# A grouped convolution: the first half image block by a plain load and a ScalarE cast, the weights on another queue

## Chip, cores, metric

One core of one Trainium2 chip. Times are device microseconds of a whole run. Every run told of here was "fast" (slow when it lies over 1.5% above the fastest of its kernel), and only such runs are compared. The sets of runs were made on chips 0, 3, 13 and 15; each set has the kernel before in its own rounds, and times are compared by the ratio to it.

## What must be computed

A 3x3 convolution in 8 groups, with padding of one pixel: x is 16 x 64 x 64 x 64, the weights are 128 x 8 x 3 x 3, the output is 16 x 128 x 64 x 64, all fp32.

```python
for g in range(8):
  for b in range(16):
    for co in range(16):
      for ci in range(8):
        for kh in range(3):
          for kw in range(3):
            output[b, 16*g + co] += weight[16*g + co, ci, kh, kw] * x_pad[b, 8*g + ci, kh:kh+64, kw:kw+64]
```

That is 16.8 MB to read and 33.6 MB to write.

## The kernel before

GpSimd issues all image loads, and they cast fp32 to bf16 on the way (16.81 MB read, 8.39 MB written by its queue, q0). SyncE issues the weights, and later the 32 stores of 1 MB. DVE multiplies the weights with a mask into E (five instructions); TensorE transposes E, DVE and ScalarE copy the result as bf16 to wN and wS. Then TensorE does two interleaved pipes of matmuls on 32x64 tiles, and ScalarE and DVE copy the filled banks to output buffers.

```python
    def load(t, row0, p0, p1, h0, h1):
        s = sem(f"ld{len(sems)}")
        nc.gpsimd.dma_start(                                  # fp32 in memory, bf16 in t: casts
            t.rearrange("p h w -> p (h w)")[p0:p1, h0 * W : h1 * W],
            xr[row0 + p0 : row0 + p1, h0 * W : h1 * W],
        ).then_inc(s, 16)
        # ... cut: landed[tile, quarter, row] = (s, 16)

    s_w = sem("w")
    nc.sync.dma_start(w_sb, weight.rearrange("co ci kh kw -> co (ci kh kw)")).then_inc(s_w, 16)
    # ... cut: memsets of mask and ident
    for h0, h1 in ((0, 32), (32, 64)):
        load(xn[0], 0, 0, 128, h0, h1)
        if h0 == 0:
            # ... cut: three affine_selects on GpSimd
        load(xs[0], 544, 0, 128, h0, h1)
        load(xs[3], 512 - 96, 96, 128, h0, h1)
    # ... cut: the other six tiles, whole

    DVE.wait((s_w, 16), m5)
    for r in range(5):
        # ... cut: e = DVE.done(tensor_mul(E part, weights, mask part))
    PE.wait(e, m4)
    # ... cut: transposes on TensorE, copies to wN (DVE) and wS (ScalarE); the matmuls

        def finish(self, st):
            # ... cut
                    eng.wait((stored[slot], 16 * uses[slot]) if uses[slot] else None, self.full[j, im])
                    free[b] = eng.done(copy(ob[slot][:, o0 : o0 + 512], banks[b]))
            # ... cut: after two sets, SyncE stores ob[slot]; 16 such buffers in rotation
```

Of the kernel before, what the change touches and what calls it, by code (L numbers as in the profile page):

```python
# [13 lines left out]
def kernel(  # L14
# [38 lines left out]
    with tc.tile_critical():  # L53
        program(nc, x, weight, out, xn, xs, ob, w_sb, mask, ident, E, wN, wS, banks)
# [29 lines left out]
def program(nc, x, weight, out, xn, xs, ob, w_sb, mask, ident, E, wN, wS, banks):  # L84
    H = W = 64
    HW, HALF, T, G, CIg, COg, R = H * W, H * W // 2, 9, 8, 8, 16, 8
    NOB = len(ob)
# [3 lines left out]
    ACT = Order(nc, nc.scalar, "act", sems)  # L91
# [3 lines left out]
    def sem(name):  # L95
        s = nc.alloc_semaphore(name)
        sems.append(s)
        return s


    xr = x.rearrange("b c h w -> (b c) (h w)")
    landed = {}

    def load(t, row0, p0, p1, h0, h1):
        s = sem(f"ld{len(sems)}")
        nc.gpsimd.dma_start(  # L106
# [3 lines that stand above are left out]
        for q in range(p0 // 32, p1 // 32):  # L110
            for h in range(h0, h1):
                landed[t.name, q, h] = (s, 16)

    s_w = sem("w")
    nc.sync.dma_start(w_sb, weight.rearrange("co ci kh kw -> co (ci kh kw)")).then_inc(s_w, 16)

    m1 = DVE.done(nc.vector.memset(mask, 1.0))  # L117
    m2 = DVE.done(nc.vector.memset(ident, 0.0))  # L118
    for h0, h1 in ((0, 32), (32, 64)):
        load(xn[0], 0, 0, 128, h0, h1)  # L120
        if h0 == 0:
            POOL.wait(m1)
            m3 = POOL.done(nc.gpsimd.affine_select(  # L123
                out=mask, in_=mask, compare_op=ALU.is_ge, fill=0.0,
                base=0, channel_multiplier=1, pattern=[[-COg, G]],
            ))
            POOL.wait(m2)
            m4 = POOL.done(nc.gpsimd.affine_select(  # L128
                out=ident, in_=ident, compare_op=ALU.not_equal, fill=1.0,
                base=0, channel_multiplier=1, pattern=[[-1, 128]],  # L130
            ))
            POOL.wait(m3)
            m5 = POOL.done(nc.gpsimd.affine_select(  # L133
                out=mask, in_=mask, compare_op=ALU.is_ge, fill=0.0,
                base=COg - 1, channel_multiplier=-1, pattern=[[COg, G]],
            ))
        load(xs[0], 544, 0, 128, h0, h1)
        load(xs[3], 512 - 96, 96, 128, h0, h1)
    for i in range(1, 4):
        load(xn[i], 128 * i, 0, 128, 0, H)  # L140
# [16 lines left out]
    for k, (wt, off) in enumerate(((wN, 0), (wS, 32))):  # L157
        for g, t0 in enumerate(range(0, T, 4)):
# [9 lines left out]
            p = PE.done(ins)  # L168
            dst = wt[:, t0 : t0 + n, :].rearrange("p t c -> p (t c)")
            eng, copy = ((DVE, nc.vector.tensor_copy), (ACT, nc.scalar.copy))[k]  # L170
# [11 lines left out]
    stored = [sem(f"st{i}") for i in range(NOB)]  # L182
    uses = [0] * NOB
# [3 lines left out]
    class Pipe:  # L187
# [53 lines left out]
        def finish(self, st):  # L241
            i, s = st // 4, st % 4
            if s % 2 == 0:
                self.slots = [(nob[0] + im) % NOB for im in range(2)]
                self.wrote = [[], []]
                nob[0] += 2
            for j in range(2):
                for im in range(2):
                    slot, b = self.slots[im], self.banks[j][im]
                    o0 = 512 * (2 * (s % 2) + j)  # L250
                    eng, copy = ((ACT, nc.scalar.copy), (DVE, nc.vector.tensor_copy))[nev[0] % 2]
                    nev[0] += 1
                    eng.wait((stored[slot], 16 * uses[slot]) if uses[slot] else None, self.full[j, im])
                    free[b] = eng.done(copy(ob[slot][:, o0 : o0 + 512], banks[b]))  # L254
                    self.wrote[im].append(free[b])
                nev[0] += 1
            nev[0] += 1
            if s % 2 == 1:
                s0 = HALF * (s // 2)
                for im in range(2):  # L260
                    slot = self.slots[im]
                    img = 2 * i + 8 * self.k + im
                    SP.wait(*self.wrote[im])
                    nc.sync.dma_start(outf[img][:, s0 : s0 + HALF], ob[slot]).then_inc(stored[slot], 16)
                    uses[slot] += 1
# [55 lines left out]
```

## Time and profile before

| | before |
|---|---|
| time, median of 3 runs | 130.17 us (130.03 to 130.27) |
| span of the profiled run | 128.2 us |
| TensorE busy | 86.9 us, done at 94 us |
| first convolution matmul | 7.92 us |
| stores issued | from 19.95 to about 99.3 us |

The page's slices tell when a unit is full. In answers of windows, each line has the stretch, its length, the busy time of five engines, TensorE's granted clock, the busy share of the 16 DMA engines, and the GB/s at the destination. A window counts each packet whole where it begins, so the edges of short windows are blurred, and shares slightly over 1 occur. The prediction shows the lines.

### The profile page before, as it was taken

The page shows a single profiled execution, that of the slowest core. Times are in us where ns is not written, and L with a number is a line of the kernel's source. Part 1 is how long each engine was busy: PE and PEld are TensorE (multiplying, and loading weights), DVE is VectorE, ACT ScalarE, POOL GpSimd, SP SyncE. Part 2 cuts the span into 40 slices and gives each one's busy share as a digit, 9 for nine tenths or more (in the row PEclk, how much of TensorE's full clock was granted, in tenths as well). Part 3 has the DMA queues.
Part 4 walks back from the last instruction along what each step waited for, and adds up shares of the span by engine and source line. Part 5 has one row for each costly group of instructions (what it writes and reads, how often), then busy time and mean ns, then how long its engine had stood idle before and what let it go on. Part 6 is the DMA issues. An engine that isn't in the chain of part 4 may idle for free.

```text
span 128.2 us, 3808 instructions
## 1 busy us (share of the span) xinstructions
PE 86.9 (68%) x2322; PEld 41.2 (32%) x1170; DVE 45.8 (36%) x74; ACT 37.0 (29%) x68; POOL 7.2 (6%) x19
## 2 busy tenths in 40 slices
PE   0199999999999999999999999999910000000000
PEld 0153353544435355444553544544500000000000
DVE  1840465446444645446544564465440000000000
ACT  4030354345333543336333453354330000000000
POOL 5960000000000000000000000000000000000000
PEclk9999999999999999999999999999996555555555
DMA  2999999999999999999999999999999999999950
GB/s 24 162 202 215 224 212 220 215 289 284 281 289 281 284 271 297 297 401 424 419 424 424 396 435 406 435 414 429 417 424 429 424 432 422 429 427 432 427 243 10
DMA packets 6271, 42.21 MB, mean 329 GB/s; under 512 B 848, under 2 KB 848, under 8 KB 1424
## 3 DMA queue, kind: packets, MB, share of 16 engines
q1 hardware_dynamic: 4752, 33.59, 62.9%
q0 software_dynamic: 1504, 8.39, 32.8%
q8 instruction: 13, 0.21, 0.6%
q14 instruction: 2, 0.02, 0.0%
HBM read 16.81 MB, written 33.55 MB: 393 GB/s over the span
## 4 chain that ended last, share of the span: by engine, by line
PE 67%; DVE 4%; issue 2%; POOL 1%; POOLq 0%; DVEq 0%; SPq 0%
PE bank L227 65%; DVE E L149 2%; DVE ob L254 2%; PE bank L162 2%; POOL ident L128 0%; POOL mask L123 0%; POOL mask L133 0%; POOL xn L106 0%; POOLq L123 0%; POOLq L316 0%; DVEq L75 0%; SPq L53 0%
## 5 line engine op out<-in xcount | busy, mean ns | idle before, releaser
L227 PE MATMUL bank<-xs,wS 32*64 32x504 bf16 (+3 forms) x1152 | 71.6, 374 | 0.6 <-issue 0.4
L227 PE MATMUL bank<-xn,wN 32*64 32x504 bf16 (+3 forms) x1152 | 71.8, 380 | 0.2 <-DVE ob L254 0.2
L254 DVE COPY ob<-bank 128x512 f32<-128x512 f32 x64 | 41.3, 686 | 45.4 <-PE bank L227 45.4
L254 ACT COPY ob<-bank 128x512 f32<-128x512 f32 x64 | 34.5, 589 | 51.2 <-PE bank L227 51.1
L222 PEld LDWEIGHTS <-wS 32*64 32x64 bf16 x576 | 27.5, 104 | 20.8 <-issue 9.9
L222 PEld LDWEIGHTS <-wN 32*64 32x64 bf16 x576 | 19.1, 106 | 25.0 <-issue 20.9
L162 PE MATMUL bank<-ident,E 128*128 128x128 bf16 x18 | 2.1, 313 | 5.9 <-DVE E L149 5.9
L106 POOL DMA_DIRECT2D xs<-in_x_dram x7 | 3.8, 543 | 0.0
L162 PEld LDWEIGHTS bank<-ident,E 128*128 128x128 bf16 x18 | 1.8, 148 | 5.9 <-DVE E L149 5.9
L149 DVE TENSOR_TENSOR E<-w_sb,mask 128x288 bf16<-128x288 f32 x5 | 2.9, 642 | 1.7 <-DMA w_sb<-in_weight_dram 1.7
L106 POOL DMA_DIRECT2D xn<-in_x_dram x5 | 2.9, 583 | 1.0 <-SPq L53 1.0
L172 ACT CAST wS<-bank 128x512 bf16<-128x512 f32 (+1 forms) x3 | 1.2, 487 | 5.2 <-PE bank L162 5.2
L172 DVE CAST wN<-bank 128x512 bf16<-128x512 f32 (+1 forms) x3 | 1.5, 551 | 0.7 <-PE bank L162 0.7
L172 ACT ACT_TABLE_LOAD x1 | 1.3, 1283 | 1.0 <-SPq L53 1.0
L117 DVE MEMSET mask<- 128x8 f32 x1 | 0.1, 65 | 1.1 <-SPq L53 1.1
L128 POOL TENSOR_SCALAR_AFFINE_SELECT ident<-ident 128x128 bf16<-128x128 bf16 x1 | 0.3, 306 | 0.0
L123 POOL TENSOR_SCALAR_AFFINE_SELECT mask<-mask 128x8 f32<-128x8 f32 x1 | 0.2, 211 | 0.1
L133 POOL TENSOR_SCALAR_AFFINE_SELECT mask<-mask 128x8 f32<-128x8 f32 x1 | 0.2, 199 | 0.0
L302 POOL MEMSET const-float32-0.0<- 128x1 f32 x1 | 0.1, 99 | 0.3 <-issue 0.3
L118 DVE MEMSET ident<- 128x64 uint32 x1 | 0.1, 112 | 0.0
L302 POOL MEMSET const-bfloat16-1.0<- 128x1 bf16 x1 | 0.1, 102 | 0.0
L302 POOL MEMSET const-uint8-127<- 128x1 uint8 x1 | 0.1, 102 | 0.0
(1 smaller groups left out, 0.1 us busy)
## 6 DMA issues: line engine op xcount, KB each, us to landing
out_dram<-ob SPq DMA_DIRECT2D x32, 1024.0 KB, 28.0
xn<-in_x_dram POOLq DMA_DIRECT2D x3, 1024.0 KB, 29.6
xs<-in_x_dram POOLq DMA_DIRECT2D x2, 1024.0 KB, 29.6
xn<-in_x_dram POOLq DMA_DIRECT2D x2, 512.0 KB, 7.6
xs<-in_x_dram POOLq DMA_DIRECT2D x2, 512.0 KB, 9.4
xs<-in_x_dram POOLq DMA_DIRECT2D x1, 768.0 KB, 48.4
xs<-in_x_dram POOLq DMA_DIRECT2D x2, 128.0 KB, 9.5
w_sb<-in_weight_dram SPq DMA_DIRECT2D x1, 36.0 KB, 1.8
```

Of the source, the lines that this page charges most:

```text
L106: nc.gpsimd.dma_start(t.rearrange("p h w -> p (h w)")[p0:p1, h0 * W : h1 * W], xr[row0 + p0 : row0 + p1, h0 * W : h1 * W],).then_inc(s, 16)
L117: m1 = DVE.done(nc.vector.memset(mask, 1.0))
L123: m3 = POOL.done(nc.gpsimd.affine_select(out=mask, in_=mask, compare_op=ALU.is_ge, fill=0.0, base=0, channel_multiplier=1, pattern=[[-COg, ...
L128: m4 = POOL.done(nc.gpsimd.affine_select(out=ident, in_=ident, compare_op=ALU.not_equal, fill=1.0, base=0, channel_multiplier=1, pattern=[ ...
L133: m5 = POOL.done(nc.gpsimd.affine_select(out=mask, in_=mask, compare_op=ALU.is_ge, fill=0.0, base=COg - 1, channel_multiplier=-1, pattern= ...
L149: e = DVE.done(nc.vector.tensor_mul(E[:, :, 32 * r : 32 * r + 32].rearrange("p t (g c) -> p t g c", c=CIg), wv.unsqueeze(2).to_broadcast([ ...
L162: ins = nc.tensor.matmul(banks[b][:, 128 * t : 128 * t + 128], E[:, t0 + t, off : off + 128], ident, start=True, stop=True,)
L172: free[b] = eng.done(copy(dst, banks[b][:, 0 : 128 * n]))
L222: pe.ldweights(w_ap, **pos)
L227: ins = pe.add_instruction(mybir.InstMatmult(name=nc.get_next_instruction_name(), engine=mybir.EngineType.PE, start_tensor_calc=k == 0, st ...
L254: free[b] = eng.done(copy(ob[slot][:, o0 : o0 + 512], banks[b]))
L302: nc = _bacc.Bacc("TRN2", target_bir_lowering=False, num_devices=1)
```

## The change

The first half of the first image block now comes as plain fp32, on the sync queue, into the sixteenth output buffer, which is idle until later. ScalarE casts it to bf16 in two pieces. The weights go to the scalar queue, since the sync queue now begins with the block. GpSimd begins with the shifted block. The intent is to have image data sooner.

```diff
+    raw = ob[NOB - 1]
+    s_raw = sem("raw")
+    nc.sync.dma_start(raw, xr[0:128, 0:HALF]).then_inc(s_raw, 16)
     s_w = sem("w")
-    nc.sync.dma_start(w_sb, ...).then_inc(s_w, 16)
+    nc.scalar.dma_start(w_sb, ...).then_inc(s_w, 16)
+    ACT.wait((s_raw, 16))
+    for h in (0, 16):
+        raw_read = ACT.done(nc.scalar.copy(
+            xn[0][:, h : h + 16, :].rearrange("p h w -> p (h w)"), raw[:, h * W : (h + 16) * W],
+        ))
+        # ... cut: landed[xn[0], quarter, row] = raw_read for these rows
     for h0, h1 in ((0, 32), (32, 64)):
-        load(xn[0], 0, 0, 128, h0, h1)
+        if h0 > 0:
+            load(xn[0], 0, 0, 128, h0, h1)
+        load(xs[0], 544, 0, 128, h0, h1)
         # ... cut: the affine_selects
-        load(xs[0], 544, 0, 128, h0, h1)
         load(xs[3], 512 - 96, 96, 128, h0, h1)
@@ finish
-   eng.wait((stored[slot], 16 * uses[slot]) if uses[slot] else None, self.full[j, im])
+   eng.wait((stored[slot], 16 * uses[slot]) if uses[slot] else raw_read, self.full[j, im])
```

More of the change, by code (lines that the diff above doesn't have):

```diff
@@ L112, in load @@
                 landed[t.name, q, h] = (s, 16)
+    raw = ob[NOB - 1]
+    s_raw = sem("raw")
+    nc.sync.dma_start(raw, xr[0:128, 0:HALF]).then_inc(s_raw, 16)
     s_w = sem("w")
-    nc.sync.dma_start(w_sb, weight.rearrange("co ci kh kw -> co (ci kh kw)")).then_inc(s_w, 16)
+    nc.scalar.dma_start(w_sb, weight.rearrange("co ci kh kw -> co (ci kh kw)")).then_inc(s_w, 16)
+    ACT.wait((s_raw, 16))
[3 more added lines that the diff above has]
+        ))
+        for q in range(4):
+            for r in range(h, h + 16):
+                landed[xn[0].name, q, r] = raw_read
     m1 = DVE.done(nc.vector.memset(mask, 1.0))
```

## The prediction

> **What bounds the kernel now.** I read the page's picture in 40 slices first, because it tells in one look which unit is full when. One slice is 128.2 / 40 = 3.2 us.
>
> ```profile
> PE   0199999999999999999999999999910000000000
> ...
> DMA  2999999999999999999999999999999999999950
> ...
> q1 hardware_dynamic: 4752, 33.59, 62.9%
> q0 software_dynamic: 1504, 8.39, 32.8%
> ...
> HBM read 16.81 MB, written 33.55 MB: 393 GB/s over the span
> ```
>
> Counting slices from 0, TensorE is busy from slice 2 to slice 28 and done in the next; the 16 DMA engines are full from slice 1 to slice 37 without a hole, and run on alone for some 30 us. (q0 carries the loads that GpSimd issues and casts to bf16, q1 the stores.) So the transfers set the end, not the matmuls. The page's chain of work gives PE 67%, but it follows instructions, and stops where the last eviction ends, at 94.7 us. The timeline of SyncE shows what comes after:
>
> ```profile
> 90.36 9.85 SPq L264 DMA_DIRECT2D out_dram<-ob  x5
> ...
> 19.95 80.26 SPq L264 DMA_DIRECT2D out_dram<-ob  x32
> ```
>
> The last of the 32 stores was issued near 99.3 us; bytes still move until about 126. A store lands 28.0 us after its issue in the median (issues part of the page), far more than 1 MB needs alone: a long queue stands in front of it. Next the rates, from windows of busy time (start:end, length, five engines, TensorE clock, DMA share, GB/s):
>
> ```profile
> 3.20:20.00 16.80, 13.93 (x298) 6.67 (x166) 7.98 (x14) 4.46 (x9) 5.42 (x11) 1.00 1.03 204
> 20.00:54.00 34.00, 33.55 (x960) 15.73 (x481) 16.80 (x26) 14.06 (x26) 0.00 (x0) 1.00 1.02 272
> ...
> 94.70:122.00 27.30, 0.00 (x0) 0.00 (x0) 0.00 (x0) 0.00 (x0) 0.00 (x0) 0.54 1.01 427
> ```
>
> Those GB/s count bytes at the destination, and a casting load reads two bytes for each that it writes: 8.39 MB on q0 against 16.81 MB read. Counted at the source, the load stage runs at 2 x 204 = 408 (2 x 215 = 430 in its full slices), the store stage at 427: one rate for both, some 424 GB/s. Then the whole program is 16.81 + 33.55 = 50.36 MB / 424 = 118.8 us of transfer, plus the time before transfers flow, plus the end. Check: first load bytes at 2.85 us (below), a slow ramp that I put at 0.8 us, 118.8 us: 122.4 us, where the DMA share indeed leaves 1.0 (0.85 in 122:123, 0.49 in the next). Some engines end later than others, and the last bytes come at about 126. The start:
>
> ```profile
> 1.02 0.38 SPq L115 DMA_DIRECT2D w_sb<-in_weight_dram  x1
> 1.51 0.67 POOL L106 DMA_DIRECT2D xn<-in_x_dram  x1 [1.00 <-SPq L53]
> ...
> 2.97 2.86 DVE L149 TENSOR_TENSOR E<-w_sb,mask 128x288 bf16<-128x288 f32 x5 [1.72 <-DMA w_sb<-in_weight_dram]
> ...
> 5.89 2.10 PE L162 MATMUL bank<-ident,E 128*128 128x128 bf16 x18 [5.89 <-DVE E L149]
> ...
> 7.92 0.13 PEld L222 LDWEIGHTS <-wN 32*64 32x64 bf16 x4 [0.20 <-DVE wN L172]
> ```
>
> The weights are issued at 1.02, land 1.8 us later, and then E (2.9 us) and the weight transposes (2.1 us) lead to the first convolution matmul at 7.92. The first image block, issued at 1.51, landed 5.7 us later at 7.2 (the fastest landing in the view of xn), so it was not what that matmul waited for. And between the weights' bytes and the image's, the DMA engines idle:
>
> ```profile
> 2.40:2.50 0.10, 0.00 (x0) 0.00 (x0) 0.00 (x0) 0.00 (x0) 0.10 (x2) 1.00 0.22 35
> 2.60:2.70 0.10, 0.00 (x0) 0.00 (x0) 0.00 (x0) 0.00 (x0) 0.10 (x2) 1.00 0.00 0
> 2.80:2.90 0.10, 0.00 (x0) 0.00 (x0) 0.00 (x0) 0.00 (x0) 0.10 (x2) 1.00 0.50 41
> ```
>
> [...] the weights' first bytes show 1.0 us after the issue (1.02 to 2.0), the image's 1.3 us (1.51 to 2.85). [...]
>
> **The change part by part.**
> 1. Bytes: the half block was read as 1.05 MB of fp32 and written as half that; now the same 1.05 MB is read and written whole. At one rate per source byte this is 1.05 / 424 = 2.5 us of transfer in both. From the queue table: q0 16.78 MB in 32.8% of 128.2 us is 399 GB/s, q1 33.59 MB in 62.9% is 417; the difference is worth 0.1 us at most. Net zero.
> 2. Start: SyncE can issue the raw load where it issued the weights, at 1.02, so image bytes should flow from about 2.0 rather than 2.85: 0.8 us earlier, and on the path, since every later byte stands behind it. While GpSimd's first load (now the shifted block) starts up at 2.85, the raw bytes already fill the engines. The old ramp moved some 0.28 MB at the destination, 0.56 at the source, in 2.85:5.0, where 2.15 x 424 = 0.91 fits: 0.8 us lost. Part of it may be filled; I count 0.4 us. Minus up to 0.2 us since the weights' packets now compete instead of using an idle gap. Sum: 0.8 + 0.4 - 0.2 = **1.0 us gained**.
> 3. ScalarE: two casts of 128x1024. From 589 ns for 512 columns and 283 for 128, 0.8 ns a column, so 1.0 us each, an estimate. ScalarE waited 5.2 us for its first weight cast: hidden.
> 4. The weights on the other queue share the engines with the raw rows. [...] I expect the weights at 4 to 6 us instead of 2.97, and the first convolution matmul at 9 to 11 instead of 7.92, the last eviction at 95.5 to 98. This lies beside the transfers: loads alone keep the engines full till the first stores, and the last store issued 2 us later still finds some 20 us of queue in front of it.
> 5. The output buffer that the raw data borrows is the sixteenth; its first eviction comes many microseconds after the cast, so the added wait is free.
>
> **The rivals.** (a) The weights' delay costs what it takes from TensorE, 2 to 3 us, so 132 to 133. For it: the page's chain runs through E and the matmuls. Against: TensorE is done 30 us before the end. It needs the DMA queue to run empty somewhere. (b) Nothing moves, 130.1: the gain at the start is eaten by the unequal end of the DMA engines, or the slow ramp belongs to the memory and comes with the first bytes of any queue. (c) A large gain, 127.5 or less, if a plain load were much cheaper than a casting one, or an earlier start of TensorE counted. But only 1/16 of the loads is touched, and 2% is 2.6 us, the whole transfer of the half block. (d) Store backlog: 16 buffers hold about 16 MB, and a reused one waits for its store; no such wait shows in the view of waits, and a later TensorE makes it rarer.
>
> **Range and chances.** 130.17 - 1.0 = 129.2 us. With no ramp filled and the weights in the way it is 129.6 or a little more; with the whole ramp filled 128.6; runs scatter by 0.1. I take 128.5 to 130.0. Faster by over 2% needs 127.57 or less, which no term supplies: 0.03. Slower by over 2% needs 132.8, rival (a): 0.02. Within 2%: 0.95.
>
> **What would show it.** Step 2: DMA share near 1 from about 2.0 us, and the fall of the DMA share at the end about 1 us earlier than 122.5. Step 1: the bytes of q1 up by 1.05 MB, those of q0 down by 0.5, source rates unchanged. Step 4: E starts after 4 us, TensorE starts and ends later, and the span shrinks all the same. [...] If a hole appears in the DMA row, or the rate in the store stage falls below 420, the prediction fails.

The sum in step 2: 0.8 + 0.4 - 0.2 = 1.0 us, and 130.17 - 1.0 = 129.2 us. The 0.8 is read from the trace (2.85 less 2.0); the 0.4 is an estimate, half of the 0.8 us that the ramp lost; the 0.2 is an estimate too, and agrees with the 0.21 us that the weights' 144 packets took in before (their times, summed, over 16 engines).

## The result

| | before | changed |
|---|---|---|
| median of 6 runs | 130.13 us (129.95 to 130.27) | 129.51 us (129.18 to 130.01) |
| ratio, 95% interval | | 0.9956 (0.9936 to 0.9977) |
| profiled span | 128.2 us | 127.9 us |

A ratio here is the mean time of one kernel's fast runs over that of the other's fast runs of the same rounds, so it is not quite the ratio of the medians. The change gains 0.44%, which is 0.57 us of 130.1. The time lies within 2%, as predicted, and a little under half of the predicted 1.0 us is missing. A second set of runs, below, gave 0.9975, where two thirds are missing.

The slices and queues of the changed kernel, from its page (queue lines: packets, MB, share of the 16 engines):

```profile
PE   0029999999999979999999999999991000000000
...
DMA  3999999999999999999999999999999999999930
...
q1 hardware_dynamic: 4752, 34.61, 65.2%
q0 software_dynamic: 1360, 7.87, 30.1%
q8 instruction: 13, 0.21, 0.6%
q10 hardware_dynamic: 144, 0.04, 0.2%
```

TensorE starts later than before, the DMA engines sooner (a 3 in the first slice where a 2 was), and they run dry a little sooner (3 in the last but one where a 5 was). The 1.05 MB of the block moved to q1, half as many bytes left q0, and the weights make up q10.

The start in the timeline of the changed kernel:

```profile
0.97 0.40 ACTq L119 DMA_DIRECT2D w_sb<-in_weight_dram  x1
1.02 0.38 SPq L117 DMA_DIRECT2D ob<-in_x_dram  x1
...
5.87 2.91 DVE L162 TENSOR_TENSOR E<-w_sb,mask 128x288 bf16<-128x288 f32 x5 [4.62 <-DMA w_sb<-in_weight_dram]
...
6.79 1.99 ACT L122 CAST xn<-ob 128x1024 bf16<-128x1024 f32 x2 [4.09 <-DMA ob<-in_x_dram]
...
10.87 0.13 PEld L235 LDWEIGHTS <-wN 32*64 32x64 bf16 x4 [0.20 <-DVE wN L185]
```

The weights, though issued at 0.97, are waited for until 5.87. TensorE starts the convolution 2.95 us later than before (10.87 against 7.92). The block itself is cast long before it is needed.

Now the DMA engines in the first microseconds and in the last ones. Before:

```profile
2.00:3.00 1.00, 0.00 (x0) 0.00 (x0) 0.03 (x1) 0.26 (x1) 0.91 (x5) 1.00 0.34 49
3.00:4.00 1.00, 0.00 (x0) 0.00 (x0) 1.00 (x2) 0.00 (x0) 1.00 (x3) 1.00 0.94 94
...
122.00:123.00 1.00, 0.00 (x0) 0.00 (x0) 0.00 (x0) 0.00 (x0) 0.00 (x0) 0.50 0.85 360
123.00:124.00 1.00, 0.00 (x0) 0.00 (x0) 0.00 (x0) 0.00 (x0) 0.00 (x0) 0.50 0.49 205
124.00:125.00 1.00, 0.00 (x0) 0.00 (x0) 0.00 (x0) 0.00 (x0) 0.00 (x0) 0.50 0.27 115
125.00:126.00 1.00, 0.00 (x0) 0.00 (x0) 0.00 (x0) 0.00 (x0) 0.00 (x0) 0.50 0.06 25
```

The changed kernel in the same windows, and one earlier at the end:

```profile
2.00:3.00 1.00, 0.00 (x0) 0.00 (x0) 0.00 (x0) 0.69 (x1) 0.91 (x5) 1.00 0.90 174
3.00:4.00 1.00, 0.00 (x0) 0.00 (x0) 0.00 (x0) 0.00 (x0) 1.00 (x3) 1.00 0.99 323
...
121.00:122.00 1.00, 0.00 (x0) 0.00 (x0) 0.00 (x0) 0.00 (x0) 0.00 (x0) 0.50 0.78 328
122.00:123.00 1.00, 0.00 (x0) 0.00 (x0) 0.00 (x0) 0.00 (x0) 0.00 (x0) 0.50 0.45 188
123.00:124.00 1.00, 0.00 (x0) 0.00 (x0) 0.00 (x0) 0.00 (x0) 0.00 (x0) 0.50 0.25 107
124.00:125.00 1.00, 0.00 (x0) 0.00 (x0) 0.00 (x0) 0.00 (x0) 0.00 (x0) 0.50 0.06 25
125.00:126.00 1.00, 0.00 (x0) 0.00 (x0) 0.00 (x0) 0.00 (x0) 0.00 (x0) 0.50 0.06 25
```

Read these from the bottom. A share of 0.06 and 25 GB/s is one engine out of 16 (427/16 = 26.7). All the shares came one microsecond earlier in the changed kernel: 0.78, 0.45, 0.25 stand at 121, 122, 123, where before had 0.85, 0.49, 0.27 at 122, 123, 124. But then one engine alone works on for two microseconds instead of one, and the last bytes come at nearly the same time. So the gain reached 15 engines, and the end is the sixteenth's. From here on this was the question: what holds the last engine?

The trace's transfer records say more than the windows. Each transfer leaves 16 records of 4 bytes (528 = 33 x 16 on q1 in before, 192 = 12 x 16 on q0), which I take as one on each engine, its last write. The trace names no engine, but rows can be followed: for 2977 of the 3433 store rows from 57 us on in before, some row or record begins exactly 3 ns before the row ends (no other offset within 30 ns has over 703), so I take this one as the next on the same engine. The records after which nothing begins are 16 in each kernel of the table, and these are the ends of the 16 engines. (The last 16 records by time are not: with nine taps the engine that ends last has two among them.) I also counted, from 57 us on, the 8 KB store rows that took 319 to 450 ns; the median row took 309. Such slow rows come singly: 12 in 4 us, where one engine moves 13, and with nine taps they average some 348 ns. Nearly all of them lie before TensorE's end (the last at 94.8 us in before).

Followed from row to row, the slow rows turn out to be those of one engine: in before no two of the 104 overlap, and 99 of them begin within 13 ns of where the one before ended, the others one or four rows later. From the last slow row on, the links lead to one end alone in before, again, w_only, w_first, raw_halves and short_mm, and it is the last one. (In the first profile of the changed kernel three ends are possible, the last among them.) So the engine that ends last is the one whose rows are slow while TensorE works. The column "excess" sums what rows of 318 to 600 ns took over 309, from 1 us after the last load landed to the last eviction (the copy that empties the last bank). The table holds the kernels of the experiments too.

```text
                     slow   instruction   excess,   ends of the 16 DMA engines, us
kernel               rows   packets       us        mean of first 15   fifteenth   last
before               104    13            4.1       123.7              125.1       126.4
w_only               108    13            4.3       123.5              125.0       126.7
changed              114    13            4.8       122.5              123.9       126.1
again (changed)      115    13            4.9       122.4              124.0       126.7
raw_halves           116    13            4.7       122.6              124.2       125.8
w_first              108    13            4.5       123.0              124.3       126.4
late15               192    13            7.4       122.6              124.2       128.5
short_mm              54    13            3.9       122.7              124.5       125.7
before_few            46     4            1.1       122.9              123.8       124.0
few_taps              47     4            1.2       121.9              122.8       122.9
few_again             49     4            1.3       121.8              122.7       122.7
late15_few            55     4            1.6       121.6              122.7       123.0
```

### The profile page after: what moved, and what is told of

Its sections match the earlier page's. It is cut to its first block, busy times and chain, and to the rows that moved or that the text cites. A ratio compares the mean times of both kernels' runs of the same rounds, so it can differ in the third digit from the quotient of the medians.

```text
span 127.9 us, 3812 instructions
## 1 busy us (share of the span) xinstructions
PE 86.4 (68%) x2322; PEld 40.5 (32%) x1170; DVE 45.9 (36%) x74; ACT 39.0 (30%) x70; POOL 6.7 (5%) x18
## 4 chain that ended last, share of the span: by engine, by line
PE 66%; DVE 4%; DMA 4%; issue 1%; ACTq 0%; DVEq 0%; SPq 0%
PE bank L240 65%; DMA w_sb<-in_weight_dram 4%; DVE E L162 2%; DVE ob L267 2%; PE bank L175 2%; ACTq L329 0%; DVEq L75 0%; SPq L53 0%
## 5 line engine op out<-in xcount | busy, mean ns | idle before, releaser
L240 PE MATMUL bank<-xn,wN 32*64 32x504 bf16 (+3 forms) x1152 | 70.9, 376 | 0.2 <-DVE ob L267 0.2
L235 PEld LDWEIGHTS <-wS 32*64 32x64 bf16 x576 | 27.0, 104 | 21.5 <-issue 10.9
L122 ACT CAST xn<-ob 128x1024 bf16<-128x1024 f32 x2 | 2.0, 1042 | 4.1 <-DMA ob<-in_x_dram 4.1
L106 POOL DMA_DIRECT2D xn<-in_x_dram x4 | 2.3, 580 | 0.0
```

The costliest lines, as they stand in the source:

```text
L106: nc.gpsimd.dma_start(t.rearrange("p h w -> p (h w)")[p0:p1, h0 * W : h1 * W], xr[row0 + p0 : row0 + p1, h0 * W : h1 * W],).then_inc(s, 16)
L122: raw_read = ACT.done(nc.scalar.copy(xn[0][:, h : h + 16, :].rearrange("p h w -> p (h w)"), raw[:, h * W : (h + 16) * W],))
L235: pe.ldweights(w_ap, **pos)
L240: ins = pe.add_instruction(mybir.InstMatmult(name=nc.get_next_instruction_name(), engine=mybir.EngineType.PE, start_tensor_calc=k == 0, st ...
```

## The experiments

My theory had become this one, called A and then C in the expectations: transfers bound the kernel and start 1.1 us sooner, but the end is that of one DMA engine which is delayed by something TensorE does. The rivals were that TensorE's late start costs time directly, that the change itself makes an engine lag, and that the last engine is late because of the loads that GpSimd issues. Where an expectation below shows a cut, a reason that no run shows was taken out; its forecast stands as the author's estimate.

**again**: the changed kernel, unaltered.

> The changed kernel once more, unaltered, for a second profile. In the first pair of profiles the transfers ran 1.1 us ahead (the fall of the DMA share from 1.0 came at about 121.3 us instead of 122.4), yet the times differ by 0.57 us in the mean, because the last of the 16 DMA engines ended only 0.25 us earlier (126.1 against 126.4). Theory A (that last engine's lag behind the others differs from run to run): ratio to before 0.993 to 0.998; the DMA share falls again near 121.3 us, and the distance from there to the last transfer is not the same 4.7 us. Theory B (the change itself makes one engine lag): the same 4.7 us or more, against 4.0 in before.

Measured: 129.93 us, ratio 0.9975 (0.9951 to 0.9998). Fifteen engines again came over 1 us sooner than in before (122.4 against 123.7), the last one at 126.7. Its distance to the fifteenth was 2.7 us, against 1.3 and 1.7 in the two kernels with the old loads. Both theories keep a part: the time differs from run to run, and the lag is larger in both profiles of the changed kernel. The two sets of runs give 0.57 and 0.33 us of gain.

**w_first**: weights ahead of the raw block on the sync queue.

```diff
+    nc.sync.dma_start(w_sb, ...).then_inc(s_w, 16)
     nc.sync.dma_start(raw, xr[0:128, 0:HALF]).then_inc(s_raw, 16)
-    nc.scalar.dma_start(w_sb, ...).then_inc(s_w, 16)
```

> The changed kernel, but the weights go first on the sync queue, ahead of the raw block[...]. Theory A ([...] TensorE's start is beside the path): weights land at 3.0 to 3.3 us instead of 5.9, first convolution matmul at 8 to 8.5 instead of 10.9, time within 0.3 us of the changed kernel's. Rival (the late TensorE start costs time that the early raw block had gained): 1 to 3 us faster than the changed kernel, ratio to before 0.98 to 0.988.

Measured: ratio 1.0000 (0.9978 to 1.0023). The weights landed 1.8 us after their issue, and the first convolution matmul came at 8.26, as theory A had it. No time was gained by TensorE's earlier start; the kernel was 0.3 us slower than the changed one of the same rounds. The raw block's issue moved from 1.02 to 1.46, and the mean of the first 15 engines lies 0.5 us later than in the changed kernel. This speaks for the transfers' start and against TensorE's, though the intervals of 1.0000 and 0.9975 overlap.

**w_only**: the kernel before, with the weights alone moved.

```diff
-    nc.sync.dma_start(w_sb, ...)
+    nc.scalar.dma_start(w_sb, ...)
```

> The kernel before, with nothing but the weights moved to the scalar queue. Theory A: nothing competes with the weights before 2.85 us, so they land at 3.0 as before and the time is before's, ratio 0.998 to 1.002. Rival (the scalar queue itself is late or slow for such rows): weights at 4 us or later.

Measured: ratio 0.9998 (0.9977 to 1.0019), the weights landed 1.9 us after their issue. Here the scalar queue is about as quick as the sync queue (1.9 against 1.8 us in before). The delay in the changed kernel (4.9 us from issue to landing) comes from the bytes beside the weights, and the move of the weights alone is worth nothing.

**late15**: the changed kernel, TensorE delayed by doing E six times.

```diff
-    for r in range(5):
+    e = None
+    for r in list(range(5)) * 6:
+        if r == 0:
+            DVE.wait(e)
```

> The changed kernel, with the making of the expanded weights done six times over, which delays TensorE by 5 x 2.9 = 14.5 us (a first convolution matmul at about 25.5 us, the last eviction at about 112). Theory A (transfers bound, TensorE has slack): the last store is issued near 113 and still finds other stores before it; time within 0.4 us of the changed kernel, ratio to before 0.993 to 0.999. Rival (TensorE's start counts): 5 to 14 us slower.

Measured: 131.71 us, ratio 1.0120 (1.0099 to 1.0140), so 1.9 us slower than the changed kernel of the same rounds. Neither side had it: a delay of 14.5 us costs 1.9. The windows show that the bulk ended nearly as before and that one engine worked on alone, longer:

```profile
123.00:124.00 1.00, 0.00 (x0) 0.00 (x0) 0.00 (x0) 0.00 (x0) 0.00 (x0) 0.50 0.25 107
124.00:125.00 1.00, 0.00 (x0) 0.00 (x0) 0.00 (x0) 0.00 (x0) 0.00 (x0) 0.50 0.06 25
...
126.00:127.00 1.00, 0.00 (x0) 0.00 (x0) 0.00 (x0) 0.00 (x0) 0.00 (x0) 0.50 0.06 25
127.00:128.00 1.00, 0.00 (x0) 0.00 (x0) 0.00 (x0) 0.00 (x0) 0.00 (x0) 0.50 0.08 33
```

The 107 GB/s at 123 to 124 are the changed kernel's; the single engine lasts until 128.5 instead of 126.1. The slow rows, which I can count only while nothing but stores moves, grew from 114 to 192 (some at the end on other engines), their excess from 4.8 to 7.4 us. The stage in which nothing but stores moves and TensorE works lasted from the landing of the last load, 45.1 us, to the last eviction, 113.4. In the changed kernel it is 53.2 to 97.5, in before 56.0 to 94.7. This led to theory C.

**few_taps**: the changed kernel with 3 of 9 taps (wrong result).

```diff
-    taps = [(1, 1)] + [(a, b) for a in range(3) for b in range(3) if (a, b) != (1, 1)]
+    taps = [(1, 1), (0, 1), (2, 1)]
+    T = 3
```

> The changed kernel with 3 of the 9 taps (a wrong result on purpose): a third of TensorE's instructions, the same loads and stores. In the five profiles so far 15 of the 16 DMA engines end within some 2.5 us of each other, and one ends 1.3 to 4.4 us after them; while only stores move and TensorE still works, the rows of one engine take 348 ns instead of 309 (104 such rows in before, 114 and 115 in the changed kernel, 192 with TensorE 14.5 us late), and none do once TensorE is done. Theory C (TensorE's instructions or work slow one DMA engine, whose lag then sets the end): slow rows fall to about a third, the last engine ends within 1 us of the fifteenth, time 2 to 3 us below the changed kernel, ratio to before 0.975 to 0.985. Theory D (the last engine is late for another reason, such as the loads that GpSimd issues): its lag of 2 us or more stays, ratio 0.993 to 1.0.

Measured: 126.42 us, ratio 0.9715 (0.9696 to 0.9734). The loads and stores are the same, yet the program is some 3 us shorter. Slow rows fell to 47, and the last engine ended 0.1 us after the fifteenth. Theory D, the loads that GpSimd issues, is out, because they are unchanged. The page of this kernel shows what else shrank:

```profile
PE 53.6 (43%) x786; PEld 17.5 (14%) x402; DVE 44.9 (36%) x74; ACT 38.4 (31%) x70; POOL 6.7 (5%) x18
...
q8 instruction: 4, 0.07, 0.2%
```

The DMA engines also carry instructions: the page lists them as a queue of their own, with 13 packets of 16 KB in the changed kernel, where TensorE has 2322 + 1170 recorded instructions, and 4 here, where it has 786 + 402. That is 269 and 297 instructions to a packet, so the packets follow the number of instructions. They cost the data time: in before each packet held one DMA engine for 0.88 to 0.98 us, and the row after it (the one that begins 14 to 24 ns before the packet ends, so taken as on the same engine) took 0.67 to 0.73 us instead of 0.31, at all seven packets from 54 us on. By these figures a packet costs one engine an estimated 1.3 us; nine packets fewer, spread over 16 engines, are 0.7 us by this estimate, and the mean of the first 15 engines came 0.7 us sooner (0.8 with the old loads). The slow engine of before has no gap at the time of any such packet from 57 us on, so its slow rows are another thing than these packets.

**short_mm**: all instructions, little streaming (wrong result).

```diff
+            if k > 0:
+                hi = lo + 1
             nr, nw = hi - lo, w1 - w0
```

> The changed kernel with all its TensorE instructions, but 8 of 9 taps cover one image row instead of eight (a wrong result on purpose): as many instructions, much less streaming. If the count of TensorE instructions[...] slows the one DMA engine: as many slow rows in total and the lag of 2 us stays, ratio to before 0.993 to 1.0. If it is the streaming of matmuls: slow rows fall to a third or less, ratio 0.975 to 0.985, as in the run with 3 taps.

From its page:

```profile
PE 57.9 (45%) x2322; PEld 34.7 (27%) x1170; DVE 45.8 (36%) x74; ACT 39.0 (31%) x70; POOL 6.7 (5%) x18
...
q8 instruction: 13, 0.21, 0.6%
```

Measured: 129.17 us, ratio 0.9931 (0.9909 to 0.9954). TensorE was busy for 57.9 us instead of 86.4 and its last bank was copied by 91 us, about as early as with 3 taps (88), but it had 13 instruction packets, and the last engine came at 125.7. So it is mainly the number of instructions, not the streaming and not the early end of TensorE, that costs the 3 us. The slow rows did not stay as many as expected: 54, not some 110, at 358 ns in the mean. They were fewer but longer, and some fell out of the count above 450 ns; their excess stayed, 3.9 us. Divided by the recorded instructions of all engines in the same stretch the excess is 2.5 ns here (3.9 us by 1533), 2.6 in before (4.1 by 1599), the changed kernel and late15, and 2.5 to 2.8 in the kernels with 3 taps. So the excess follows the number of instructions and not the streaming, and it, not the count of slow rows, is the better measure of the delay.

**skip15**: the last store in two parts, of 120 and 8 rows, to relieve one engine, "engine 15" in the expectation, by an estimated 2 us or so. Which engines get which rows was assumed, not shown.

```diff
-   nc.sync.dma_start(outf[img][:, s0 : s0 + HALF], ob[slot]) ...
+   for p0, p1 in ((0, 120), (120, 128)):        # for the very last store only
+       nc.sync.dma_start(outf[img][p0:p1, s0 : s0 + HALF], ob[slot][p0:p1]) ...
```

> The changed kernel, but the very last store is split into 120 and 8 partitions. [...] If engine 15 is the one that ends last: the end comes 1.5 to 2 us earlier, ratio to before 0.980 to 0.985. If it is another engine: no gain, ratio 0.995 to 1.001.

Measured: 130.54 us, ratio 1.0031 (1.0008 to 1.0054): no gain, so the engine that was to be relieved is not shown to be the last. q1 has 535 records instead of 528, so the two parts left 23 where one store left 16; that fits 15 + 8, if each part leaves one record on each engine that moves it. The last two 4-byte records came at 126.7 and 127.0 us with one row between them on the same engine, so it seems that the engine that ended last had received one of the 8 extra rows. The trace does not name a row's engine, so which one it is stays open. In this profile the weights landed 2.6 us after their issue, though the start of the kernel is the changed one's (4.9 us): their delay is not fixed.

**before_few** and **few_again**: the kernel before and the changed kernel, both with 3 taps (wrong results), in the same rounds. The edit is that of few_taps.

> The kernel before with 3 of the 9 taps (a wrong result on purpose): before, without most of TensorE's instructions. With 3 taps the changed kernel came to 0.9715 of before, all 16 DMA engines ending within 1.7 us. Theory C (the start gains 1.1 us for all transfers; in the full kernel half of it is lost again at the last DMA engine, which TensorE's instructions delay): without that delay the full gain shows, ratio to before 0.979 to 0.982, that is 0.8 to 1.1% over the changed kernel with 3 taps. Rival (the change is worth only 0.3 to 0.6 us at any rate): within 0.5% of the changed kernel with 3 taps, ratio 0.974 to 0.976.

> The changed kernel with 3 of the 9 taps once more (a wrong result on purpose), in the same rounds as the kernel before with 3 taps, to compare the two: ratio to before 0.970 to 0.973.

Measured: 127.46 us, ratio 0.9803 (0.9776 to 0.9830), for before with 3 taps; 126.22 us, ratio 0.9707 (0.9686 to 0.9728), for the changed kernel with 3 taps. The medians differ by 1.24 us, the ratios by 1.0% (0.9707 / 0.9803 = 0.9902). With most of TensorE's instructions gone, the change gives what its start promised, two to four times what it gives in the full kernel (0.57 and 0.33 us). The end of the changed kernel with 3 taps:

```profile
121.00:122.00 1.00, 0.00 (x0) 0.00 (x0) 0.00 (x0) 0.00 (x0) 0.00 (x0) 0.50 0.62 262
122.00:123.00 1.00, 0.00 (x0) 0.00 (x0) 0.00 (x0) 0.00 (x0) 0.00 (x0) 0.50 0.12 49
123.00:124.00 1.00, 0.00 (x0) 0.00 (x0) 0.00 (x0) 0.00 (x0) 0.00 (x0) 0.50 0.00 0
```

No engine is left alone: all 16 end by 122.7.

**raw_halves**: the raw block as two transfers with rows of 4 KB.

```diff
-    nc.sync.dma_start(raw, xr[0:128, 0:HALF]).then_inc(s_raw, 16)
+    for n in range(2):
+        # shortened: n-th half of the columns
+        nc.sync.dma_start(raw[:, half], xr[0:128, half]).then_inc(s_raw[n], 16)
```

> The changed kernel with the raw block fetched as two transfers of 4 KB rows instead of one of 8 KB rows. [...] the weights land at 3.8 to 4.5 us instead of 5.9, and the first convolution matmul comes at 9 to 9.5 instead of 10.9. If the weights are late because all raw bytes go first: 5.9 as before. Time: TensorE earlier by 1.5 us moves the last DMA engine by 0.1 to 0.2 us at most, ratio to before 0.993 to 0.998.

Measured: 129.56 us, ratio 0.9960 (0.9941 to 0.9979). E could start at 5.30 instead of 5.87, so the weights came 0.6 us sooner, not 1.4 to 2.1 us; the first convolution matmul came at 10.3. In short_mm, whose start is the changed one's, E could start at 5.40, so even 0.6 us is not clear of the scatter. The 3.8 to 4.5 us expected for the weights missed, and together with the 2.6 us in skip15 this leaves open how the weights' rows and the raw block's share the engines. The time is the changed kernel's.

**late15_few**: late15 with 3 taps (wrong result; both edits as above).

> The changed kernel with TensorE 14.5 us late and 3 of the 9 taps (a wrong result on purpose). With 9 taps the delay cost 2.0 us or 1.4% (1.012 of before against 0.9975), and the last DMA engine came at 128.6 us instead of 126.1 to 126.7. Theory C [...]: with 3 taps most of the cost goes, ratio to before 0.970 to 0.975, the last DMA engine within 1 us of the fifteenth. Rival (a late TensorE delays the stores themselves): the 1.4% stays, ratio 0.983 to 0.987.

Theory C, in measured terms: a late TensorE costs only because more of its instructions then meet stores alone, and so the last engine is delayed more.

Measured: 126.43 us, ratio 0.9698 (0.9680 to 0.9716). The 14.5 us of delay cost nothing at all (0.9707 without it). A late TensorE does not delay the stores as such.

## Why the prediction was right, and where a size was off

- **Bound.** Right. Transfers set the end: 14.5 us of delay on TensorE cost 1.9 us, and none with few instructions.
- **Step 1, bytes.** Right: q1 gained 1.02 MB net of the departed weights, q0 lost 0.52 MB, and the store stage still runs at 421 to 427 GB/s.
- **Step 2, the start.** Right: bytes flow at 0.90 of the engines from 2.0 us, and the first 15 engines end 1.1 us sooner (123.7 to 122.5). The packet records put the first image bytes at 2.09 us instead of 2.89 (2.0 and 2.85 in the prediction), so the 0.8 us was right. Counted in bytes at the source and at 424 GB/s, the changed kernel was 0.9 us ahead at 10 us and 1.1 at 60 us. How much of that the filled ramp gave and the weights took (+0.4 and -0.2) can't be read apart; their sum was small, as predicted. With 3 taps the whole gain shows, 1.24 us.
- **Step 3, the casts.** Right: 1042 ns each, and ScalarE still waited 1.7 us for its first weight cast.
- **Step 4, the weights.** Its numbers held: E from 5.87, convolution from 10.87, last eviction at 97.5. Its reason no run shows: the test of it, raw_halves, missed. The remark that this "lies beside the transfers" held less well, as the next point says.
- **Step 5, the borrowed buffer.** Right: no wait for the casts appears at the evictions.
- **The term that was mis-sized** is the end. The prediction let the unequal end of the engines stand as it was ("Some engines end later than others, and the last bytes come at about 126") and carried the 1.0 us through to it. The last engine moved only from 126.4 and 126.7 in the two profiles with the old loads to 126.1, 126.7 and 125.8 in the three with the new: from a mean of 126.5 to 126.2, while the other 15 moved by 1.1 us. The times give 0.57, 0.33 and, for the variant in halves, 0.52 us. Rival (b), that the unequal end eats the gain, was half true.
- **Why the last engine lags more.** Shown by the runs: the lag goes away with the number of TensorE's instructions, with either start (the last engine 0.0 to 0.3 us behind the fifteenth with 3 taps, 1.2 to 4.3 with nine), and it grows to cost 1.9 us when TensorE works later. Shown by the rows: one engine is slowed by 2.5 to 2.8 ns for each recorded instruction while nothing but stores moves, whatever the taps and the streaming. The change has the loads end 2.8 us sooner and TensorE end 2.8 us later, so the stage in which instructions meet stores alone is 44.3 us long instead of 38.7. The excess of the slow engine in it rose from 4.1 and 4.3 us with the old loads to 4.8, 4.9 and 4.7 with the new. That is some 0.6 us more, and the last engine gained 0.3 us where the others gained 1.1. Profiles of one kernel scatter by 0.6 us at the last engine, so a finer account isn't possible here. Not shown is what goes with each instruction and slows that engine; it isn't the instruction packets, which the rows place on other engines. Every run has a span and a clock, so instructions were recorded in all of them; whether the recording itself does it was not tested. How the slow engine fares while loads and stores mix is not read either.

## What to carry to other kernels

Where DMA engines are full from start to end, as here, an earlier start of the first bytes carries through to the bulk: 0.8 us at the start became 1.1 at the end of 15 engines. A delay of TensorE by 14.5 us did not hold up the bulk (122.6 against 122.5). Look then at the last two windows of the profile: a share of 1/16 means that a single engine sets the end, and a gain for the other 15 does not shorten the program by as much. In a program of thousands of unrolled TensorE instructions (3492 recorded here), their number can then matter to the end of the transfers; here taking two thirds of them away brought 2.6 to 3.3 us of 130, some 0.7 of it on all engines and the rest on the last one.

Moving a load to another queue does not settle when it lands. 36 KB of weights, issued beside a 1 MB load from another queue, landed 4.7 to 4.9 us after their issue in most profiles instead of the 1.8 to 1.9 of before, w_only and w_first, and in two with the same start 4.4 (short_mm) and 2.6 (skip15). From the start of the issuing instruction to the first recorded bytes it took 1.0 us for the weights from SyncE and 1.4 us for the casting load from GpSimd in before, and 0.6 and 0.7 us from its end.
